# Expert weights in pieces of twice the size, and the arena they live in laid out anew

## The chip, the cores and the metric

The kernel runs on one core of one Trainium2 chip. The metric is device time in microseconds (us), the median of the runs of one kernel. A core has five engines with an instruction sequence each: PE (TensorE, matrix products; its weight loads are listed apart as PEld), DVE (VectorE), ACT (ScalarE), POOL (GpSimd) and SP (SyncE, which here only issues DMAs). They meet through semaphores. Data come from HBM into SBUF (128 partitions) by DMA; matrix products end in PSUM.

## The reference

One decoder block on 256 tokens of width 2048, all in float32. Cut to what matters:

```python
h    = rms_norm(x, norm_mix_g)
proj = h @ w_in                                  # 2048 x 7168
x    = x + concat([moba_attention(q, k, v), hgrn2(q, f, i, g)]) @ w_out
h2   = rms_norm(x, norm_ffn_g)
# router: best of 4 groups, best 2 of its 4 experts -> combine[token, expert]
for e in range(16):                              # 2048 -> 1024 -> 2048
    a, u = h2 @ w_gate[e], h2 @ w_up[e]
    hid  = silu(a) * u * combine[:, e]
    out  = out + hid @ w_down[e]
y    = rms_norm(x + out, final_norm_g)
```

The 16 experts have three matrices of 8 MB each, 24 MB an expert and 384 MB in all. Every one is read once.

## The kernel before

**Front part (0 to about 494 us).** X is normed and transposed, fourteen in-projections and one out-projection run as float32 split into a high and a low half (three products), with attention and HGRN worked off between them from a queue of small steps. The projection weights come in pieces of 1 MB called `raw` (`issue_raw`, L97), two buffers of them. `units()` splits each into two `whl` tiles: ACT copies the high half (L262), DVE subtracts to get the low half (L263), PE uses both. After chosen units (`ahead`) it also issues the load of a piece of expert weights.

**Experts.** Tokens of one expert are gathered into 64 places. For expert e, PE does, in the order of the code: the gate products `ga` (`stream`, L823), the up products `up` (also L823), the scatter of the expert before (L811 into a `psc` buffer, of which there are two, then L813 on DVE adds it into `acc`), a scatter matrix (two transposes, L798), the gather of the next expert (L775 from X into `psc`, L777 on ACT copies to `xn`, L783 transposes, L786 on DVE scales into `xg`), the transposes of `hid` (L871, copied by DVE at L872), and the down products `pd` (L880, copied out by ACT at L883). That is program order; a scheduler then sets the order on each engine, and it weaves L811, L775 and L783 between the products of the next expert. The last expert's down products run in column blocks of 512 (L893 to L913), each followed by its scatter and by the final norm's sums.

**The last norm's gain.** `final_gain()` spreads the 2048 gains of the final norm over all partitions by 16 small matmuls (`pt<-frow`, L836) and four ACT copies (L838). It is called in expert 15, between gate and up.

**Weights.** A matrix is cut into 8 pieces of 1 MB, 8 KB in each partition, loaded by SP (L233 for gate and up, L236 for down; L242 for the last expert's down). SBUF has an arena of 22 slots of 8 KB per partition, `area(s)`. In the front part they hold `hT`, `oT`, attention and HGRN buffers, `raw` and `whl`; each becomes a weight slot when its last front tenant is done. The first 22 pieces go into the 22 slots (`first`); three of these become `acc` (two) and `work` in expert 0, and the other 19 form a ring (`cycle`). When PE has used a piece, `advance()` issues the next load into the slot that has come free.

Of the kernel before, what the change touches and what calls it, by code (L numbers as in the profile page):

```python
# [19 lines left out]
P = 128  # L20
T = 256
# [16 lines left out]
def hybrid_block_kernel(  # L38
# [19 lines left out]
    def area(s, shape, dtype=F32, name="ar"):  # L58

        return arena.tile(shape, dtype, name=name, tag=f"a{s}")  # L60

    def pair(s, name):
        t = area(s, [P, 2, 1024], name=name)
        return t[:, 0], t[:, 1]
# [116 lines left out]
    hTh = [area(0 + i, [P, 8, T], F32R, name="hTh") for i in range(2)]  # L181
    hTl = [area(2 + i, [P, 8, T], F32R, name="hTl") for i in range(2)]
    oTh = [area(4 + i, [P, 8, T], F32R, name="oTh") for i in range(2)]
    oTl = [area(6 + i, [P, 8, T], F32R, name="oTl") for i in range(2)]
# [37 lines left out]
    def slot_of(idx):  # L222
        return first[idx] if idx < NSLOT else cycle[(idx - NSLOT) % len(cycle)]

    def load():
        nonlocal nxt
        e, kind, i = pieces[nxt]
        wt = area(slot_of(nxt), [P, 2048], name="wt")
        if kind < 2:

            src = (w_gate, w_up)[kind][0, e].rearrange("(b p q) f -> p b q f", p=P, q=4)
            q = 2 * (i % 2)
            nc.sync.dma_start(out=wt.rearrange("p (a b) -> p a b", a=2),  # L233
                              in_=src[:, i // 2, q:q + 2, :])
        elif e < NE - 1:
            nc.sync.dma_start(out=wt, in_=w_down[0, e, i * P:(i + 1) * P, :])  # L236
        else:
            b, hf = i // 2, i % 2
            k = 4 if b < 3 else 2
            for a in range(0, 4, k):  # L240
                r0 = (hf * 4 + a) * P
                nc.sync.dma_start(  # L242
                    out=wt.rearrange("p (a b) -> p a b", a=4)[:, a:a + k],
                    in_=w_down[0, e, r0:r0 + k * P, b * 512:(b + 1) * 512].rearrange(
                        "(c p) f -> p c f", p=P))
        loaded[nxt] = wt
        nxt += 1
# [3 lines left out]
    ahead = {12, 20, 100, 104}  # L251
    ahead |= {112 + u for u in (1, 3, 6, 8, 11, 13, 16, 18, 21, 23, 26, 30)}

    def units():
# [5 lines left out]
        for hf in range(2):  # L260
            t = area(19 + unit % 3, [P, 2, k, 1024 // k], F32R, name="whl")
# [296 lines left out]
    def att_block(g, a, hook=None):  # L558
        later = {}
        kT, qT = map(heads, pair(a[0], "kq"))  # L560
        vA, s1 = pair(a[1], "vs")
# [8 lines left out]
        bgq.append(attention(g, qT, kT, s1, area(a[2], [P, 2048], name="asc"), later))  # L570
# [5 lines left out]
    def rec_block(g, a):  # L576
        later = {}
        f, k = map(heads, pair(a[0], "fk"))
# [9 lines left out]
        q, qs = map(heads, pair(a[1], "qq"))  # L588
# [3 lines left out]
        AT, vv = pair(a[2], "av")  # L592
        AT = AT.rearrange("p (h n t) -> p h n t", h=4, n=NT)
        vv = tiles(vv)
        o, sg = pair(a[3], "os")
        later["o_"] = o.rearrange("p (n h e) -> p n h e", n=NT, h=4)
        bgq.append(hgrn(f, k, q, AT, area(a[4], [P, 1536], name="rsc"), later))
# [12 lines left out]
    att_block(0, (8, 9, 10), h_chunks)  # L610
    att_block(1, (11, 12, 13))
    rec_block(0, (14, 8, 9, 10, 11))
    rec_block(1, (12, 13, 14, 8, 9))
# [41 lines left out]
    while nxt < NSLOT:  # L655
        load()
# [96 lines left out]
    def advance():  # L753
        if nxt < len(pieces):
            load()

    def piece(e, kind, i):
        return loaded.pop((e * 3 + kind) * 8 + i)
# [57 lines left out]
    def stream(ps, xg, e, kind):  # L816
        for i in range(8):
            wt = piece(e, kind, i)
            for k in range(2):
                c = 2 * i + k  # L820
                for z in range(2):
                    o = k * 1024 + z * 512
                    mm(ps[64 * z:64 * z + 64], xg[:, c], wt[:, o:o + 512],  # L823
                       start=c == 0, stop=c == NC - 1)
            advance()

    out_v = out[0].rearrange("(n p) d -> p n d", p=P)
    fs = cst.tile([P, NT, 4], F32, name="fs")
    def final_gain():
        sl = [slot_of((NE - 1) * 24 + i) for i in (5, 6, 7)]  # L830
        gf = area(sl[0], [P, D], name="gf")
        y = [area(sl[1 + n], [P, D], name=f"y{n}") for n in range(NT)]
# [6 lines left out]
        return sl, gf, y  # L839
# [5 lines left out]
    for e in range(NE):  # L845
# [17 lines left out]
        V.tensor_tensor(hid, hid, up, ALU.mult)  # L863
        if pend is not None:
            scatter(*pend)
# [4 lines left out]
        for j in range(4):  # L870
            nc.tensor.transpose(pt[:, j], hid[:, j * P:(j + 1) * P], ident)  # L871
        V.tensor_copy(hT, pt)  # L872
        pd = pq.tile([P, 2, 512], F32, name="pd")
        if e < NE - 1:
            for i in range(8):
                wt = piece(e, 2, i)
                z, j = i // 4, i % 4
                for blk in range(4):
                    lo = 64 * (blk % 2)
                    mm(pd[lo:lo + 64, blk // 2], hT[:, j, z * 64:z * 64 + 64],  # L880
                       wt[:, blk * 512:(blk + 1) * 512], start=i == 0, stop=i == 7)
                advance()
# [4 lines left out]
    osl = osb.rearrange("p j (k f) -> p (j k) f", k=2)  # L887
    for b in range(4):
        for hf in range(2):
            wt = piece(NE - 1, 2, 2 * b + hf).rearrange("p (c f) -> p c f", c=4)  # L890
# [36 lines left out]
    with tc.If(nover > CAP):  # L927
        with tc.tile_pool(name="ovp", bufs=1, space=PSUM) as ovp:
            free = [s for s in range(NSLOT) if s not in alias + sl]
            h2T = [area(free.pop(), [P, 8, T], name="h2T") for _ in range(2)]  # L930
            oc = small8[:, 6:8]
            for n in range(NT):
                xs = area(free.pop(), [P, D], name="xs")
                V.tensor_scalar(xs, x2[:, n], r2[:, n:n + 1], None, ALU.mult)
                for c in range(NC):
                    pt = ovp.tile([P, P], F32, name="pt", tag="pt", bufs=2)
                    nc.tensor.transpose(pt, xs[:, c * P:(c + 1) * P], ident)
                    V.tensor_scalar(h2T[c // 8][:, c % 8, n * P:(n + 1) * P], pt,
                                    gffn[:, c:c + 1], None, ALU.mult)
            hTo = area(free.pop(), [P, 8, T], name="hTo")  # L940
            hd = area(free.pop(), [P, NT, 512], name="hd")
            wts = [area(free.pop(), [P, 4, 512], name="wto") for _ in range(4)]
            yo = [area(free.pop(), [P, D], name="yo") for _ in range(NT)]
            with tc.For_i(0, NE, 1) as e:
# [12 lines left out]
                for fb in range(2):  # L957
                    for kind, src in ((0, w_gate), (1, w_up)):
                        ps = ovp.tile([P, NT, 512], F32, name="ps", tag="ps", bufs=2)
                        for c in range(0, NC, 4):  # L960
                            wt = rows4(src, c, fb * 512)
                            for k in range(4):
                                for n in range(NT):
                                    mm(ps[:, n], h2T[c // 8][:, c % 8 + k, n * P:(n + 1) * P],
# [58 lines left out]
```

## Time and profile before

| | us |
|---|---|
| runs | 1428.54, 1429.59, 1430.69 (median 1429.59) |
| profiled execution | 1428.93, with a span of 1427.2 |
| front part, 0 to 494 | PE 483.29 busy, DMA share 0.61 |
| experts 3 to 14, 653 to 1335 | 682.00 long, PE 644.89 busy, PEld 215.21, DMA share 1.01, 421 GB/s |
| the end, 1335 to 1427 | PE 73.27 busy, DMA share 0.85 |

PE carries 94% of the chain that ended last, and its granted clock over the span is 0.996 of full speed, so PE ran at 2.4 GHz. "Idle before" in the rows is the time an engine stood still before a group, with the operation that ended it in the bracket. The matmul rows of the timeline count hardware instructions: one matmul of 512 float32 columns has two of them, one of 128 columns has one.

### The profile page before, as it was taken

What the parts mean: (1) busy time and instruction counts of PE and PEld (TensorE: products, weight loads), DVE (VectorE), ACT (ScalarE), POOL (GpSimd) and SP (SyncE); (2) the same over time, 40 slices, a digit from 0 to 9 for tenths busy, and PEclk for the clock granted to TensorE, in tenths of its full rate; (3) what the DMA queues carried; (4) which work ended last, traced back from release to release, by engine and by line L of the source; (5) the groups of instructions that cost most, each with busy time, mean ns of one, the idle gap of its engine ahead of it and who ended that gap; (6) DMA issues with size and microseconds to landing.
All of it is one profiled execution on the core that took longest, in us unless ns stands there. A gap on an engine that the chain in (4) does not pass through costs nothing.

```text
span 1427.2 us, 16870 instructions
## 1 busy us (share of the span) xinstructions
PE 1357.8 (95%) x7073; PEld 737.6 (52%) x7073; DVE 439.8 (31%) x714; ACT 273.7 (19%) x408; POOL 18.0 (1%) x47
## 2 busy tenths in 40 slices
PE   7999999999999999999999999999999999999995
PEld 6999898898887633433332332323323333233333
DVE  4554557557555410221112111111111111211012
ACT  5453543533533300000000000000000000000012
POOL 2000000000000000000000000000000000000002
PEclk9999999999999999999999999999999999999998
DMA  6566553555697699999999999999999999999995
GB/s 229 186 210 169 162 176 120 176 177 178 219 343 292 228 384 418 422 421 422 420 421 422 421 422 421 422 420 421 421 422 422 420 422 421 421 421 421 421 413 214
DMA packets 111648, 483.79 MB, mean 339 GB/s; under 512 B 19728, under 2 KB 21968, under 8 KB 63440
## 3 DMA queue, kind: packets, MB, share of 16 engines
q1 hardware_dynamic: 110912, 482.62, 85.5%
q8 instruction: 57, 0.93, 0.3%
q14 instruction: 23, 0.19, 0.0%
q10 hardware_dynamic: 656, 0.04, 0.0%
HBM read 480.54 MB, written 2.10 MB: 338 GB/s over the span
## 4 chain that ended last, share of the span: by engine, by line
PE 94%; DVE 2%; ACT 1%; issue 1%; DMA 0%; SPq 0%; DVEq 0%; ACTq 0%
PE ga L823 16%; PE up L823 16%; PE pd L880 15%; PE psc L811 7%; PE pp L310 5%; PE pp L312 5%; PE pp L311 5%; PE pp L293 4%; PE pp L295 4%; PE pp L296 4%; PE psc L775 4%; PE pt L783 1%; PE pw L414 1%; PE pd L893 1%; ACT work L883 1%
## 5 line engine op out<-in xcount | busy, mean ns | idle before, releaser
L823 PE MATMUL ga<-wt,xg 128*64 128x512 f32 x1024 | 272.3, 601 | 0.0
L823 PE MATMUL up<-wt,xg 128*64 128x512 f32 x1024 | 228.0, 595 | 0.0
L263 DVE TENSOR_TENSOR whl<-raw,whl 128x1024 fp32r<-128x1024 f32 x144 | 175.6, 1224 | 136.1 <-ACT whl L262 135.9
L880 PE MATMUL pd<-wt,work 128*64 128x512 f32 x960 | 210.0, 594 | 4.0 <-DVE work L872 4.0
L262 ACT ACTIVATE whl<-raw 128x1024 fp32r<-128x1024 f32 x144 | 152.0, 1058 | 233.4 <-PE pp L312 121.5
L813 DVE TENSOR_TENSOR acc<-acc,psc 128x512 f32<-128x512 f32 x112 | 74.4, 686 | 378.3 <-PE psc L811 378.3
L823 PEld LDWEIGHTS ga<-wt,xg 128*64 128x64 f32 x1024 | 78.8, 136 | 149.0 <-issue 139.8
L293 PE MATMUL pp<-hTh,whl 128*128 128x256 f32 x512 | 147.7, 288 | 3.1 <-ACT hTh L328 3.1
L295 PE MATMUL pp<-hTl,whl 128*128 128x256 f32 x512 | 146.5, 286 | 0.9 <-DVE hTl L329 0.9
L296 PE MATMUL pp<-hTh,whl 128*128 128x256 f32 x512 | 146.2, 286 | 0.0
L823 PEld LDWEIGHTS up<-wt,xg 128*64 128x64 f32 x1024 | 72.5, 137 | 135.0 <-issue 127.7
L880 PEld LDWEIGHTS pd<-wt,work 128*64 128x64 f32 x960 | 69.2, 137 | 134.3 <-issue 123.9
L811 PE MATMUL psc<-work,pT 64*128 64x512 f32 x240 | 99.7, 642 | 16.5 <-ACT work L883 15.4
L293 PEld LDWEIGHTS pp<-hTh,whl 128*128 128x128 f32 x512 | 99.4, 194 | 4.2 <-ACT hTh L328 4.0
L295 PEld LDWEIGHTS pp<-hTl,whl 128*128 128x128 f32 x512 | 99.4, 194 | 1.5 <-DVE hTl L329 1.4
L296 PEld LDWEIGHTS pp<-hTh,whl 128*128 128x128 f32 x512 | 99.4, 194 | 0.0
L883 ACT ACTIVATE work<-pd 128x1024 f32<-128x1024 f32 x15 | 15.3, 1023 | 429.0 <-PE pd L880 429.0
L775 PE MATMUL psc<-X,pg 128*64 128x512 f32 x256 | 94.8, 596 | 0.7 <-DVE pg L767 0.7
L863 DVE TENSOR_TENSOR work<-work,up 128x512 f32<-128x512 f32 x16 | 11.0, 687 | 244.4 <-PE up L823 244.4
L777 ACT ACTIVATE xn<-psc 128x512 f32<-128x512 f32 x32 | 19.0, 595 | 308.2 <-PE psc L775 308.2
L310 PE MATMUL pp<-whl,hTh 128*128 128x512 f32 x192 | 77.6, 404 | 0.0
L312 PE MATMUL pp<-whl,hTl 128*128 128x512 f32 x192 | 75.4, 393 | 0.0
(240 smaller groups left out, 1054.7 us busy)
## 6 DMA issues: line engine op xcount, KB each, us to landing
wt<-in_w_gate_dram SPq DMA_DIRECT2D x128, 1024.0 KB, 19.8
wt<-in_w_up_dram SPq DMA_DIRECT2D x128, 1024.0 KB, 19.8
wt<-in_w_down_dram SPq DMA_DIRECT2D x126, 1024.0 KB, 19.8
raw<-in_w_in_dram SPq DMA_DIRECT2D x55, 1024.0 KB, 5.2
raw<-in_w_out_dram SPq DMA_DIRECT2D x16, 1024.0 KB, 5.3
X<-in_x_dram SPq DMA_DIRECT2D x4, 512.0 KB, 7.1
wt<-in_w_down_dram SPq DMA_DIRECT2D x4, 512.0 KB, 11.4
out_dram<-y SPq DMA_DIRECT2D x4, 512.0 KB, 4.3
```

Source lines behind the costliest of these rows:

```text
L262: S.activation(t[:, 0], raw[:, k * hf:k * hf + k], AF.Copy)
L263: V.tensor_tensor(t[:, 1], raw[:, k * hf:k * hf + k], t[:, 0].bitcast(F32), ALU.subtract)
L293: mm(o, hi[:, k, cs], ah, start=st and j % 2 == 0, stop=False, skip_group_check=True)
L295: mm(o, hi[:, k, cs], al, start=False, stop=False, skip_group_check=True)
L296: mm(o, lo[:, k, cs], ah, start=False, stop=sp, skip_group_check=True)
L310: mm(pp[:, n], ah, hi[:, k], start=c == c0, stop=False)
L312: mm(pp[:, n], al, hi[:, k], start=False, stop=c == c1 - 1)
L775: mm(ps[64 * z:64 * z + 64], pg[:, n], x2[:, n, b * 512:(b + 1) * 512], start=n == 0, stop=n == 1)
L811: mm(ps, pT[lo:lo + 64, n], osb[lo:lo + 64, j], start=True, stop=True)
L813: V.tensor_tensor(acc[n][:, bs], x2[:, n, bs] if e == 0 else acc[n][:, bs], ps, ALU.add)
L823: mm(ps[64 * z:64 * z + 64], xg[:, c], wt[:, o:o + 512], start=c == 0, stop=c == NC - 1)
L880: mm(pd[lo:lo + 64, blk // 2], hT[:, j, z * 64:z * 64 + 64], wt[:, blk * 512:(blk + 1) * 512], start=i == 0, stop=i == 7)
```

## The change

The expert weights come in pieces of 2 MB: four to a matrix, 16 KB in each partition. In gate and up, a partition's four rows of a block are now one load; in down, the rows of a half matrix are dealt to the partitions in fours (`p j` where it was `j p`), so that two neighbouring rows lie in one stretch, and `hid` is transposed with every fourth column (`p j`) to fit. The arena has ten slots of 16 KB (`double`) and two of 8 KB (`single`). Twelve loads (22 MB) go out early: eight after units in the front part (where sixteen did), four behind it. The ring has nine doubles (18 MB), where it had 19 singles (19 MB). `acc[0]` and `work` share a double, `acc[1]` is a single that is freed in expert 1. `final_gain()` runs in expert 1 rather than 15, into the other single.

```diff
+    shared = {k: double(k, [P, 2, 2048], name=f"sh{k}") for k in (1, 2, 3, 8)}
...
-            raw = area(17 + i % 2, [P, k, w], name="raw")
+            raw = half((8, i % 2)).rearrange("p (k w) -> p k w", k=k)
...
-    pieces = [(e, kind, i) for e in range(NE) for kind in range(3) for i in range(8)]
-    first = [15, 16, 10, 11, 0, 1, 2, 3, 12, 13, 9, 14, 8, 4, 6, 17, 18, 5, 7, 19, 20, 21]
-    NSLOT = len(first)
-    alias = first[13:16]
-    cycle = [s for s in first if s not in alias]
+    pieces = [(e, kind, i) for e in range(NE) for kind in range(3) for i in range(4)]
+    early_loads = [(1, 0), (2, 1), (3, 4), (4, 5), (5, 2), (6, 3), (0, 0, 0), (7, 6),
+                   (8, 8), (9, 9), (10, 7), (0, 1, 1)]
+    ring = [d[1] for d in early_loads if len(d) == 2 and d[0] != 7]
+    late_loads = [(11, 0, 0), (11, 1, 1)] + [(n, ring[(n - 12) % 9]) for n in range(12, len(pieces))]
...
+        if kind < 2:
+            return (w_gate, w_up)[kind][0, e].rearrange("(b p q) f -> p b q f", p=P, q=4)[
+                :, i, a:b, :]
+        return w_down[0, e].rearrange("(z p j) d -> p z j d", p=P, j=4)[
+            :, i // 2, i % 2 * 2 + a:i % 2 * 2 + b, :]
...
+        wt = double(at[0], [P, 2, 2048], name="wt")
+        loaded[idx] = [wt[:, 0], wt[:, 1]]
+        if e < NE - 1 or kind == 0:
+            nc.sync.dma_start(out=wt.rearrange("p h (a b) -> p (h a) b", a=r // 2),
+                              in_=source(idx, 0, r))
...
-    ahead = {12, 20, 100, 104}
-    ahead |= {112 + u for u in (1, 3, 6, 8, 11, 13, 16, 18, 21, 23, 26, 30)}
+    ahead = {12, 102, 113, 117, 122, 127, 131, 136}
...
     def stream(ps, xg, e, kind):
-        for i in range(8):
-            wt = piece(e, kind, i)
-            for k in range(2):
-                c = 2 * i + k
+        for i in range(4):
+            for h, wt in enumerate(piece(e, kind, i)):
+                for k in range(2):
+                    c = 4 * i + 2 * h + k
...
-            advance()
+            if (e, kind, i) not in ((0, 0, 0), (0, 1, 3)):
+                advance()
...
-        if e == NE - 1:
-            sl, gf, y = final_gain()
+        if e == 1:
+            gf = final_gain()
...
-            for n in range(NT):
-                acc[n] = area(alias[n], [P, D], name=f"acc{n}")
-            work = area(alias[2], [P, 2048], name="work")
+            rest = double(6, [P, 2, D], name="rest")
+            acc[0] = rest[:, 0]
+            work = rest[:, 1]
...
-            nc.tensor.transpose(pt[:, j], hid[:, j * P:(j + 1) * P], ident)
+            nc.tensor.transpose(pt[:, j], hid.rearrange("s (p j) -> s j p", j=4)[:, j], ident)
...
+    yt = double(late_loads[-9][1], [P, NT, D], name="y")
```

The order of the instructions moves with it, since the scheduler places PE's small work by the loads. On PE, in one of the experts 3 to 14, the stretch from the scatter of the expert before (L811) over the gate products to the transposes of the gathered tokens (L783) reads before:

```order
L880 MATMUL pd<-wt,work 64x512 x32
L811 MATMUL psc<-work,pT 128x512
L823 MATMUL ga<-wt,xg 64x512 x4
L811 MATMUL psc<-work,pT 128x512
L823 MATMUL ga<-wt,xg 64x512 x4
L811 MATMUL psc<-work,pT 128x512 x2
L823 MATMUL ga<-wt,xg 64x512 x4
L811 MATMUL psc<-work,pT 128x512 x2
...
L775 MATMUL psc<-X,pg 64x512
L783 MATMUL pt<-ident,xn 128x128 x4
L823 MATMUL up<-wt,xg 64x512 x4
L783 MATMUL pt<-ident,xn 128x128 x4
```

The same stretch on PE now (L848 is the scatter, L860 the products, L812 the gather, L820 its transposes, L921 the down products; `rest` holds `work`):

```order
L921 MATMUL pd<-wt,rest 64x512 x32
L848 MATMUL psc<-rest,pT 128x512 x2
L860 MATMUL ga<-wt,xg 64x512 x8
L848 MATMUL psc<-rest,pT 128x512 x4
L860 MATMUL ga<-wt,xg 64x512 x8
L848 MATMUL psc<-rest,pT 128x512 x2
L812 MATMUL psc<-X,pg 64x512
L860 MATMUL ga<-wt,xg 64x512 x8
L812 MATMUL psc<-X,pg 64x512 x6
L860 MATMUL ga<-wt,xg 64x512 x8
L812 MATMUL psc<-X,pg 64x512
L820 MATMUL pt<-ident,xn 128x128 x8
```

The eight scatter products went in six places of one or two; they now go in three places of two, four and two, with eight gate products between, and the eight transposes stand in one row where four up products parted them.

On SP, in the out-projection of the front part, the pieces of `raw` (L97) and of expert weights (L233) stand before as:

```order
L97 DMA raw<-in_w_out_dram 128x4x512 x3
L233 DMA wt<-in_w_gate_dram 128x2048
L97 DMA raw<-in_w_out_dram 128x4x512
L233 DMA wt<-in_w_gate_dram 128x2048
L97 DMA raw<-in_w_out_dram 128x4x512
```

and now on SP (`sh_73` is the shared double that holds both `raw` buffers):

```order
L111 DMA sh_73<-in_w_out_dram 128x4x512 x3
L267 DMA wt<-in_w_gate_dram 128x4096
L111 DMA sh_73<-in_w_out_dram 128x4x512 x2
L267 DMA wt<-in_w_up_dram 128x4096
L111 DMA sh_73<-in_w_out_dram 128x4x512 x2
```

Where one 1 MB weight piece stood between two `raw`, one of 2 MB stands between every second or third pair.

## Rows read from the trace of the kernel before

**Rows 1.** The page, part 1: busy time, share of the span, instructions.
```profile
PE 1357.8 (95%) x7073; PEld 737.6 (52%) x7073; DVE 439.8 (31%) x714; ACT 273.7 (19%) x408; POOL 18.0 (1%) x47
```

**Rows 2.** Timeline of PE, one expert: start, us, engine, line, operation, [idle before].
```profile
870.74 13.95 PE L880 MATMUL pd<-wt,work 128*64 128x512 f32 x64 [0.34 <-DVE work L872]
885.88 1.12 PE L811 MATMUL psc<-work,pT 64*128 64x512 f32 x2 [1.18 <-ACT work L883]
886.93 1.94 PE L823 MATMUL ga<-wt,xg 128*64 128x512 f32 x8
888.80 1.12 PE L811 MATMUL psc<-work,pT 64*128 64x512 f32 x2
...
891.72 1.13 PE L811 MATMUL psc<-work,pT 64*128 64x512 f32 x4
...
901.55 0.64 PE L775 MATMUL psc<-X,pg 128*64 128x512 f32 x1
...
910.33 0.75 PE L783 MATMUL pt<-ident,xn 128*128 128x128 f32 x4
911.01 1.94 PE L823 MATMUL up<-wt,xg 128*64 128x512 f32 x8
...
927.41 0.63 PE L871 MATMUL pt<-ident,work 128*128 128x128 f32 x4 [1.61 <-DVE xg L786]
...
928.82 1.51 PE L880 MATMUL pd<-wt,work 128*64 128x512 f32 x6 [0.34 <-DVE work L872]
```

**Rows 3.** Timeline of SP, the same experts: issues of eight loads of down.
```profile
890.25 17.72 SPq L236 DMA_DIRECT2D wt<-in_w_down_dram  x8
949.88 17.71 SPq L236 DMA_DIRECT2D wt<-in_w_down_dram  x8
```

**Rows 4.** Waits of PE's weight loads, 560 to 1300: total, times, longest.
```profile
PEld ga L823 <- DMA wt<-in_w_up_dram: 8.8, 13, 0.8
```

**Rows 5.** Timelines of SP and PE at the end of the last expert.
```profile
1370.33 28.55 SPq L242 DMA_DIRECT2D wt<-in_w_down_dram  x10
1408.49 3.67 PE L893 MATMUL pd<-wt,work 128*64 128x256 f32 x32
```

**Rows 6.** The page, part 6: median us from issue to landing.
```profile
wt<-in_w_down_dram SPq DMA_DIRECT2D x4, 512.0 KB, 11.4
```

**Rows 7.** DMA, 600 to 1300, and GB/s in 40 slices of 1370 to 1428.
```profile
DMA packets 40454, 294.79 MB, mean 421 GB/s; under 512 B 4493, under 2 KB 4493, under 8 KB 4493
GB/s 418 429 418 412 424 412 429 407 400 420 387 384 390 386 381 388 387 387 388 388 387 383 331 254 223 155 49 0 6 0 11 0 11 76 396 401 407 178 6 0
```

**Rows 8.** Timeline of PE, experts 1 and 2: the scatter.
```profile
570.07 1.13 PE L811 MATMUL psc<-work,pT 64*128 64x512 f32 x4
571.97 1.72 PE L811 MATMUL psc<-work,pT 64*128 64x512 f32 x4 [0.77 <-DVE acc L813]
...
617.26 1.13 PE L811 MATMUL psc<-work,pT 64*128 64x512 f32 x4
...
631.78 3.60 PE L775 MATMUL psc<-X,pg 128*64 128x512 f32 x16
```

**Rows 9.** Timeline of ACT, the end of one gather.
```profile
910.89 0.59 ACT L777 ACTIVATE xn<-psc 128x512 f32<-128x512 f32 x1
```

**Rows 10.** Timeline of PE, experts 14 and 15.
```profile
1334.01 0.63 PE L871 MATMUL pt<-ident,work 128*128 128x128 f32 x4 [1.62 <-DVE xg L786]
...
1352.09 1.12 PE L811 MATMUL psc<-work,pT 64*128 64x512 f32 x2 [1.18 <-ACT work L883]
...
1376.56 13.90 PE L823 MATMUL up<-wt,xg 128*64 128x512 f32 x64
```

**Rows 11.** Timelines of SP and ACT, and the tile `raw`, out-projection.
```profile
398.85 0.37 SPq L97 DMA_DIRECT2D raw<-in_w_out_dram  x1
404.66 1.06 ACT L262 ACTIVATE whl<-raw 128x1024 fp32r<-128x1024 f32 x1 [1.66 <-PE pp L312]
DMA to landing us min/median/max: 5.0/5.4/6.4
```

More of the change, by code (lines that the diff above doesn't have):

```diff
@@ L246, in load @@
-        loaded[nxt] = wt
-        nxt += 1
+        idx, *at = loads[nxt]
+        nxt += 1
+        e, kind, i = pieces[idx]
+        r = 4 if kind < 2 else 2
+        if len(at) == 2:
+            hf, s = at
+            wt = single(s, [P, 2048], name="wt")
+            nc.sync.dma_start(out=wt.rearrange("p (a b) -> p a b", a=r // 2),
+                              in_=source(idx, hf * r // 2, (hf + 1) * r // 2))
+            loaded.setdefault(idx, [None, None])[hf] = wt
+            return
+        wt = double(at[0], [P, 2, 2048], name="wt")
@@ new lines, in load @@
+        loaded[idx] = [wt[:, 0], wt[:, 1]]
+        if e < NE - 1 or kind == 0:
+            nc.sync.dma_start(out=wt.rearrange("p h (a b) -> p (h a) b", a=r // 2),
+                              in_=source(idx, 0, r))
+        elif kind == 1:
+            for hf in range(2):
+                nc.sync.dma_start(out=wt[:, hf].rearrange("p (a b) -> p a b", a=2),
+                                  in_=source(idx, 2 * hf, 2 * hf + 2))
+        else:
+            src = w_down[0, e].rearrange("(z p j) d -> p z j d", p=P, j=4)
+            for hf in range(2):
+                k = 4 if i < 3 else 2
+                for a in range(0, 4, k):
+                    nc.sync.dma_start(
+                        out=wt[:, hf].rearrange("p (a b) -> p a b", a=4)[:, a:a + k],
+                        in_=src[:, hf, a:a + k, i * 512:(i + 1) * 512])
@@ L569, in att_block @@
         V.tensor_tensor(qT, ps, rBh, ALU.mult)
-        bgq.append(attention(g, qT, kT, s1, area(a[2], [P, 2048], name="asc"), later))
+        bgq.append(attention(g, qT, kT, s1, half(a[2]), later))
         ps = proj_n(hTh, hTl)
@@ L591, in rec_block @@
         V.tensor_tensor(q, q, qs, ALU.mult)
-        AT, vv = pair(a[2], "av")
+        AT, vv = pair(a[2])
         AT = AT.rearrange("p (h n t) -> p h n t", h=4, n=NT)
         vv = tiles(vv)
-        o, sg = pair(a[3], "os")
+        o, sg = pair(a[3])
         later["o_"] = o.rearrange("p (n h e) -> p n h e", n=NT, h=4)
-        bgq.append(hgrn(f, k, q, AT, area(a[4], [P, 1536], name="rsc"), later))
+        bgq.append(hgrn(f, k, q, AT, half(a[4]), later))
         ps = proj_n(hTh, hTl)
@@ L753, in advance @@
     def advance():
-        if nxt < len(pieces):
+        if nxt < len(loads):
             load()
     def piece(e, kind, i):
-        return loaded.pop((e * 3 + kind) * 8 + i)
+        return loaded.pop((e * 3 + kind) * 4 + i)
     def pscr(tag="psc"):
@@ L829, in final_gain @@
     def final_gain():
-        sl = [slot_of((NE - 1) * 24 + i) for i in (5, 6, 7)]
-        gf = area(sl[0], [P, D], name="gf")
-        y = [area(sl[1 + n], [P, D], name=f"y{n}") for n in range(NT)]
+        gf = single(1, [P, D], name="gf")
         for q in range(4):
@@ L863, in hybrid_block_kernel @@
         V.tensor_tensor(hid, hid, up, ALU.mult)
+        if e == 1:
+            acc[1] = single(0, [P, D], name="acc1")
         if pend is not None:
@@ L874, in hybrid_block_kernel @@
         if e < NE - 1:
[L875 to L882, printed above, removed]
+            for i in range(4):
+                for h, wt in enumerate(piece(e, 2, i)):
+                    z, j = i // 2, i % 2 * 2 + h
+                    for blk in range(4):
+                        lo = 64 * (blk % 2)
+                        mm(pd[lo:lo + 64, blk // 2], hT[:, j, z * 64:z * 64 + 64],
+                           wt[:, blk * 512:(blk + 1) * 512], start=i + h == 0, stop=i + h == 4)
+                if (e, i) != (0, 3):
+                    advance()
             S.activation(osb, pd, AF.Copy)
@@ L928, in hybrid_block_kernel @@
         with tc.tile_pool(name="ovp", bufs=1, space=PSUM) as ovp:
-            free = [s for s in range(NSLOT) if s not in alias + sl]
-            h2T = [area(free.pop(), [P, 8, T], name="h2T") for _ in range(2)]
+            free = [d for d in ring if d != late_loads[-9][1]]
+            h2 = double(free.pop(), [P, NC, T], name="h2T")
             oc = small8[:, 6:8]
+            xss = double(free.pop(), [P, NT, D], name="xs")
             for n in range(NT):
-                xs = area(free.pop(), [P, D], name="xs")
+                xs = xss[:, n]
                 V.tensor_scalar(xs, x2[:, n], r2[:, n:n + 1], None, ALU.mult)
```

102 lines of the change are left out of this document (52 added, 50 removed).

## The prediction

> **What bounds the kernel now.** I read the busy shares first, then the timeline of one expert, then the queue that brings the weights, then the end. PE is busy for 95% of the span, so the reader looks for what PE waits for and what paces it [rows 1]. In experts 3 to 14 all is periodic: the down products begin at 870.74 in one expert and at 928.82 in the next, so the period is 58.08 us [rows 2]. Inside it PE stands still in four places, 1.18 us before the scatter (ACT copies the down products out), 1.61 before the hid transposes (a late release by DVE's gather), 0.34 before the down products, none of them for a weight. Only PE's weight loads, which run ahead of PE, waited for pieces, in the worst group 13 times in 740 us and never over 0.8 us [rows 4].
>
> The queue is nevertheless full: two issues of down lie 59.63 us apart, which is 24 MB at 2.485 us per MB [rows 3], 421 GB/s [rows 7]. DMA is thus 59.63 - 58.08 = 1.55 us an expert slower than PE and lives off the 22 MB that were loaded ahead. This lead is just used up at the end: the last 512 KB are issued at 1370.33 + 28.55 = 1398.88 and land about 11.4 later [rows 5, 6], at 1410.3; the second half of the last block's down products, which needs them, starts at 1408.49 + 3.67/2 = 1410.3 [rows 5]. So PE sets the time, with DMA level with it only at the last half block. A faster DMA alone buys nothing; a slower or later one costs at once.
>
> **The change part by part.** The sum is made against the profiled execution, 1428.93; the median of the runs is 0.66 above that.
>
> *The transfers.* The same bytes in stretches of 16 KB. The traces show 8 KB stretches at 421 GB/s, and 2 KB stretches (the last expert's down) at about 387 [rows 7]. Per engine (one of 16) a stretch of 8 KB takes 311 ns and one of 2 KB 84.7, so 6 KB cost 226.6 and about 9 ns are fixed; one of 16 KB would take 614 ns, 427 GB/s. That is an estimate: 1.5% less, 58.7 to 58.9 us an expert, still not below PE, and over the 900 us in which the queue is full about 13 us earlier at the end. Cashed: 0, since PE is the bound. Bounds: 421 GB/s (if the stretch is cut into 8 KB again) gives 0 as well, but then the lead decides, below.
>
> *The scatter and gather in one expert (12 experts, 3 to 14).* A scatter product of 512 columns uses half the rows, and two in a row run beside each other: a place with one product occupies 886.93 - 885.88 = 1.05, and the rows of one and of two are as long, 1.12 and 1.13 [rows 2]. Four gate products take 888.80 - 886.93 = 1.87; eight in one row about 3.58, since the change of work costs some 0.16 once and a product 0.43. Before, from the first scatter product to the first gather product: 901.55 - 885.88 = 15.67. After, places of two, four and two. The four have only two buffers: in expert 1, where the scatter stands in one row, the next pair starts 571.97 - 570.07 = 1.90 after the first, waiting 0.77 for DVE's add [rows 8]. So 1.06 + 3.58 + (1.90 + 1.65) + 3.58 + 1.90 (a pair, and the gather product behind it waits for a buffer) + 1.71 (four gate products, to come to the same count) = 15.38. That is -0.29 an expert. Bounds: if no buffer wait shows, 15.38 - 0.84 - 0.84 - 0.6 = 13.1, -2.6; if the pairs' waits all come on top, +0.6. I take -0.29, since the row that it rests on is this very sequence: 12 x -0.29 = -3.5.
>
> *The transposes of the gathered tokens.* Four stood before four up products and four behind, so that ACT's second copy to `xn`, 910.89 to 911.48, lay under PE's work [rows 2, 9]. Eight in a row: the first four end by 911.01, the second four wait for that copy, 0.5 with its release, less 0.1 for one change of work less: +0.4 an expert, 12 x 0.4 = +4.8. The cover of four up products (1.87) is what is lost. Bounds 0 and +0.6.
>
> *hid transposes with a stride.* The `xn` transposes, which also take every fourth column, last 0.75 where the hid ones last 0.63 [rows 2]: +0.12 x 16 = +1.9. Bounds 0 and 0.25 each.
>
> *Expert 2.* The scatter stands among the up products. From its first product to the gather 631.78 - 617.26 = 14.52 in five places of two, one, two, two and one with 4 up products between [rows 8]; now three, four and one with eight between. The three and the four each wait for buffers, 2 x 0.84 and more: about 16.4, +1.9. Bounds 0 and 3.
>
> *The gain row.* It goes from expert 15 to expert 1. Expert 14: transposes to scatter took 1352.09 - 1334.01 = 18.08 [rows 10]; elsewhere (928.82 - 927.41) + (885.88 - 870.74) = 16.55 [rows 2], so 1.5 is saved. Expert 15: from the scatter to the up products 1376.56 - 1352.09 = 24.47 [rows 10]. Without the row and with the scatter in twos and fours, 1.06 + 3.58 + 3.55 + 3.58 + 1.06 + 6.9 (16 more gate products) + 0.4 = 20.2: -4.3. In expert 1 the same sixteen small products come to the path, with no work between them: +4.3. Sum -1.5.
>
> *The early loads.* In the out-projection a `raw` is used 404.66 - 398.85 = 5.8 us after its issue, and it lands in 5.4 [rows 11]. Behind a load of 2 MB it would take about 2.3 us more. But ACT's split stands 1.66 behind PE each time [rows 11], and with three split buffers PE holds some 3 us of work in hand: cost 0. If that cover is gone, up to 1 us for each of the seven loads there, +7.
>
> *The lead.* The ring is 18 MB, not 19, and a slot comes free after 2 MB. Where the queue has to wait for a slot, in expert 0, its start can be up to 3 MB later: 3 x 2.485 = 7.5 us. Against it stand the estimated 13 us of the faster stretch: cost 0.
>
> Sum: -3.5 + 4.8 + 1.9 + 1.9 - 1.5 = +3.6, so 1432.5 for the profiled execution and **1433** for the median.
>
> **A rule that speaks against my reading.** The rows show PE busy for 95% and its weight loads for 52% of the span [rows 1]. The Trainium skill, "Perfetto Trace Analysis", section Identifying the Most-Contended Engine, holds that matmul busy share does not tell how near TensorE is to its limit and that the share of weight loads does; by that share PE would have slack, and the full queue would be the bound. By my sum the time is 1433, by that rule it is rival A. The period of 58.08 with no matmul waiting for a weight [rows 2, 4] is against it here.
>
> **The rivals.**
> *A, DMA is the bound.* Then PE's terms vanish in the slack and the 13 us of the faster stretch are gained: 1428.93 - 13.2 + 0.66 = 1416. For it: a full queue and a lead that is just used up [rows 3, 5]. Against it: no weight wait of PE in 740 us. 0.07.
> *B, PE's small waits overlap better.* The scatter in twos and fours loses no buffer wait (-2.6 in place of -0.29 in 12 experts would be -31 and is not credible in full, since a gather product behind needs the same two buffers); a third of it, -0.9 an expert, moves the sum by -7 to about 1426. For it: the places of two are free of cost beside those of one [rows 2]. Against it: the wait of 0.77 in expert 1 [rows 8]. 0.2.
> *C, slower by the lead.* The stretch is cut into 8 KB pieces, the rate stays at 421, and the later start (up to 7.5 us) comes out at the last half block, where there is no slack now [rows 5, 6]. PE's own 3.6 hide as much of it: 1428.93 + 0.66 + 7.5 = 1437. It decides once the late start passes 3.6 us. 0.16.
> *D, the stretch brings no rate and the lead holds.* The time is that of my forecast, 1433, but the queue's period stays 59.63. It is held within the forecast.
>
> **How the numbers follow.** Forecast with D 0.57, A 0.07, B 0.2, C 0.16. The forecast's own range is 1429 to 1437: its terms have bounds of some -3 and +4 together when they don't all fall to one side. To hold 8 in 10 I go down through most of B, to 1422, and up over C, to 1440. About 0.2%, 2.9 us, is what a measurement of this kernel can tell from no change: 1426.7 to 1432.5. Faster: A and some 0.13 of B and a little of the forecast, 0.25. Same: the rest of B and a third of the forecast, 0.27. Slower: 0.48.
>
> **What would show it.** In the trace after: the period of experts 3 to 14 (58.2 by my sum); the scatter's second pair waiting near 0.77 for `acc`; the second four `xn` transposes idle near 0.5 behind ACT; hid transposes of 0.75; no matmul waiting for a weight DMA; the queue at 427 GB/s (or at 421, D); 16.4 us in expert 2; the gain row in one 4.3 us block in expert 1. I am wrong if the period falls below 57.8 (B), if matmuls wait for weights in the last experts (C), or if the end comes 10 us earlier (A).

## The result, and the profile after

The changed kernel takes 1437.04 us (median of 4 runs, 1436.37 to 1437.77), the kernel before 1429.32: a ratio of 1.0053, interval 1.0036 to 1.0070. It is slower, as forecast, and lies 4 us above the 1433 of the forecast. The profiled execution took 1436.37, its span is 1434.6: 7.4 more than before.

The page after, part 1, and the timeline of PE in one expert, which answers to [rows 1, 2]:

```profile
PE 1337.6 (93%) x7073; PEld 735.7 (51%) x7073; DVE 437.1 (30%) x714; ACT 274.1 (19%) x408; POOL 17.8 (1%) x47
```

```profile
879.40 0.72 PE L912 MATMUL pt<-ident,rest 128*128 128x128 f32 x4 [1.62 <-DVE xg L823]
...
880.91 13.95 PE L921 MATMUL pd<-wt,rest 128*64 128x512 f32 x64 [0.43 <-DVE rest L913]
896.04 1.13 PE L848 MATMUL psc<-rest,pT 64*128 64x512 f32 x4 [1.18 <-ACT rest L925]
897.10 3.65 PE L860 MATMUL ga<-wt,xg 128*64 128x512 f32 x16
900.69 1.13 PE L848 MATMUL psc<-rest,pT 64*128 64x512 f32 x4
902.59 1.72 PE L848 MATMUL psc<-rest,pT 64*128 64x512 f32 x4 [0.77 <-DVE acc L850]
...
909.72 0.64 PE L812 MATMUL psc<-X,pg 128*64 128x512 f32 x1 [0.77 <-DVE acc L850]
...
920.23 0.75 PE L820 MATMUL pt<-ident,xn 128*128 128x128 f32 x4
921.43 0.75 PE L820 MATMUL pt<-ident,xn 128*128 128x128 f32 x4 [0.45 <-ACT xn L814]
```

The two waits of 0.77 for a scatter buffer, the 0.45 behind ACT's copy, and the longer hid transposes stand where the forecast put them. From the first scatter product to the gather it is 909.72 - 896.04 = 13.68, and 1.71 for four gate products that now follow: 15.39, against 15.38 forecast.

What was not in the forecast is PE's clock. The timeline of PE in expert 1, and windows on PE around the end of the gain row (columns: us, PE busy, granted clock, DMA share, GB/s):

```profile
557.53 3.88 PE L875 MATMUL pt<-frow,ident 16*128 16x128 f32 x32
561.34 15.65 PE L860 MATMUL up<-wt,xg 128*64 128x512 f32 x64
```

```profile
560.90:561.40 0.50, 0.50 (x7) 0.98 1.00 426
561.40:563.00 1.60, 1.60 (x5) 0.50 1.05 451
563.00:564.70 1.70, 1.70 (x6) 0.50 1.02 434
564.70:565.20 0.50, 0.50 (x4) 0.91 0.84 360
565.20:570.00 4.80, 4.80 (x26) 1.00 1.01 427
```

Behind 3.8 us of the 16 small products of the gain row, which fill 16 of the array's 128 rows, the granted clock is 0.50 (1.2 GHz) for 3.4 us; the 32 up products take 15.65 in place of 13.90 [rows 10]. The profile has one more such fall, at 1056.3 to 1059.7, at the head of the down products of an expert, straight behind the stretch in which PE waits 1.62, transposes, and waits 0.43:

```profile
1055.80:1056.30 0.50, 0.50 (x4) 1.00 1.00 426
1056.30:1058.00 1.70, 1.70 (x8) 0.50 0.97 414
1058.00:1059.60 1.60, 1.60 (x8) 0.50 1.11 471
```

Each costs 3.4 / 2 = 1.7 us. The profile of before has none between 17 us and the quiet tail, which begins at 1416. I call the span less half of this time at half clock (the tail left out) the span at full clock: 1427.2 before, 1434.6 - 3.4 = 1431.2 after, 4.0 more.

The queue, over 600 to 1300, and in 40 slices of 1370 to 1434, which answer to [rows 7]; and SP's loads of down, to [rows 3]:

```profile
DMA packets 20558, 299.42 MB, mean 428 GB/s; under 512 B 2281, under 2 KB 2281, under 8 KB 2281
```

```profile
GB/s 415 420 410 407 410 397 385 381 385 389 385 389 381 387 388 388 376 260 218 138 23 10 0 0 0 0 0 0 0 0 5 0 10 0 10 325 402 407 187 5
```

```profile
894.90 19.70 SPq L267 DMA_DIRECT2D wt<-in_w_down_dram  x4
953.18 19.70 SPq L267 DMA_DIRECT2D wt<-in_w_down_dram  x4
```

Half as many packets move at 428 GB/s (427 forecast), and the issues lie 58.28 apart, which is PE's period. The queue runs dry at about 1405, and PE reaches the last half block at 1417.6: the level finish of before became 12 us of slack, and none of it shortens the run. Among PE's waits from 560 to 1430 there is none of a product for a DMA.

### The profile page after: what moved, and what is told of

The parts are those of the page before. It is cut to its first block, busy times and chain, and to the rows that moved or that the text cites. A ratio compares the mean times of both kernels' runs of the same rounds, so it can differ in the third digit from the quotient of the medians.

```text
span 1434.6 us, 16513 instructions
## 1 busy us (share of the span) xinstructions
PE 1337.6 (93%) x7073; PEld 735.7 (51%) x7073; DVE 437.1 (30%) x714; ACT 274.1 (19%) x408; POOL 17.8 (1%) x47
## 4 chain that ended last, share of the span: by engine, by line
PE 92%; DVE 3%; ACT 2%; issue 1%; DMA 0%; SPq 0%; ACTq 0%; DVEq 0%
PE up L860 16%; PE ga L860 16%; PE pd L921 15%; PE psc L848 5%; PE pp L346 5%; PE pp L347 5%; PE pp L348 5%; PE pp L329 4%; PE pp L331 4%; PE pp L332 4%; PE psc L812 4%; DVE acc L850 1%; PE pw L450 1%; PE pd L937 1%; ACT rest L925 1%
## 5 line engine op out<-in xcount | busy, mean ns | idle before, releaser
L860 PE MATMUL ga<-wt,xg 128*64 128x512 f32 x1024 | 252.9, 596 | 0.0
L860 PE MATMUL up<-wt,xg 128*64 128x512 f32 x1024 | 226.1, 597 | 0.0
L921 PE MATMUL pd<-wt,rest 128*64 128x512 f32 x960 | 211.0, 597 | 5.5 <-DVE rest L913 5.5
L299 DVE TENSOR_TENSOR whl<-sh,whl 128x1024 fp32r<-128x1024 f32 x144 | 175.5, 1224 | 132.3 <-ACT whl L298 125.1
L298 ACT ACTIVATE whl<-sh 128x1024 fp32r<-128x1024 f32 x144 | 152.0, 1058 | 232.8 <-PE pp L348 110.1
L860 PEld LDWEIGHTS ga<-wt,xg 128*64 128x64 f32 x1024 | 78.5, 136 | 145.2 <-issue 143.2
L860 PEld LDWEIGHTS up<-wt,xg 128*64 128x64 f32 x1024 | 72.8, 138 | 142.7 <-issue 140.0
L921 PEld LDWEIGHTS pd<-wt,rest 128*64 128x64 f32 x960 | 67.9, 138 | 139.9 <-issue 129.9
L850 DVE TENSOR_TENSOR rest<-rest,psc 128x512 f32<-128x512 f32 x56 | 36.1, 684 | 252.5 <-PE psc L848 252.5
L848 PE MATMUL psc<-rest,pT 64*128 64x512 f32 x240 | 78.9, 641 | 28.1 <-ACT rest L925 15.4
L925 ACT ACTIVATE rest<-pd 128x1024 f32<-128x1024 f32 x15 | 15.4, 1024 | 434.5 <-PE pd L921 434.5
L812 PE MATMUL psc<-X,pg 128*64 128x512 f32 x256 | 83.3, 596 | 10.0 <-DVE acc L850 9.3
L346 PE MATMUL pp<-whl,hTh 128*128 128x512 f32 x192 | 77.5, 404 | 0.0
L347 PE MATMUL pp<-whl,hTh 128*128 128x512 f32 x192 | 74.9, 390 | 0.0
```

What stands on the lines that cost most here:

```text
L298: S.activation(t[:, 0], raw[:, k * hf:k * hf + k], AF.Copy)
L299: V.tensor_tensor(t[:, 1], raw[:, k * hf:k * hf + k], t[:, 0].bitcast(F32), ALU.subtract)
L346: mm(pp[:, n], ah, hi[:, k], start=c == c0, stop=False)
L347: mm(pp[:, n], ah, lo[:, k], start=False, stop=False)
L812: mm(ps[64 * z:64 * z + 64], pg[:, n], x2[:, n, b * 512:(b + 1) * 512], start=n == 0, stop=n == 1)
L848: mm(ps, pT[lo:lo + 64, n], osb[lo:lo + 64, j], start=True, stop=True)
```

## The experiments

Two theories. **P**: PE's own sequence sets the time, and it lost 4 us by the terms of the sum and the rest by falls of its clock. **L**, rival C of the prediction: the coarser loads and the smaller ring set it. Each version ran in 5 rounds beside the kernel before (ring7 in 1). "Half clock" is the time at 1.2 GHz in the profiled execution, without the quiet tail; "clock" the mean over all runs (37 of the kernel before, beside the versions). Small differences between two spans say little: before_02 and before_fill64 have the front part of the kernel before, and the three profiles reach the first gate product at 494.13, 493.67 and 492.98, with the whole difference made in the first 44 us.

| | median | ratio, interval | clock | span | half clock | span at full clock |
|---|---|---|---|---|---|---|
| before | 1429.3 | | 0.995 | 1427.2 | 0 | 1427.2 |
| after | 1437.0 | 1.0036 to 1.0070 | 0.9935 | 1434.6 | 6.8 | 1431.2 |
| gain_parts | 1437.3 | 1.0037 to 1.0061 | 0.993 | 1435.8 | 10.2 | 1430.7 |
| halves | 1436.9 | 1.0037 to 1.0067 | 0.9925 | 1431.4 | 3.4 | 1429.7 |
| hid_rows | 1438.0 | 1.0034 to 1.0063 | 0.992 | 1437.5 | 17.1 | 1429.0 |
| two_dmas | 1438.0 | 1.0047 to 1.0071 | 0.992 | 1436.3 | 13.6 | 1429.5 |
| four_back | 1432.6 | 0.9999 to 1.0023 | 0.993 | 1431.0 | 10.2 | 1425.9 |
| before_02 | 1439.4 | 1.0045 to 1.0078 | 0.992 | 1437.6 | 10.2 | 1432.5 |
| fill | 1458.1 | 1.0171 to 1.0209 | 0.994 | 1459.8 | 13.6 | 1453.0 |
| four_fill | 1452.8 | 1.0136 to 1.0173 | 0.995 | 1452.7 | 6.8 | 1449.3 |
| fill64 | 1453.9 | 1.0158 to 1.0186 | 0.994 | 1453.7 | 6.8 | 1450.3 |
| before_fill64 | 1447.7 | 1.0112 to 1.0142 | 0.9955 | 1448.1 | 6.8 | 1444.7 |
| best | 1441.9 | 1.0075 to 1.0105 | 0.9945 | 1438.7 | 0 | 1438.7 |
| ring7 | 1439.0 | 1.0048 to 1.0085 | 0.992 | 1439.3 | 17.1 | 1430.7 |

**gain_parts.** The gain row in four parts.

```diff
...
-        if e == 1:
-            gf = final_gain()
+        if e >= 1:
+            final_gain(e - 1)
```

`final_gain` now builds a quarter of the row, four of the 16 products, in each of experts 1 to 4.

> The changed kernel, with the gain row of the last norm built in four parts of four small products, one behind the gate products of each of experts 1 to 4. Theory P (PE's own sequence sets the time, and the clock fell to about half for 3.4 us behind the 3.81 us of small products in expert 1, which cost 1.75 us there): no part is long, the up products of expert 1 take 13.9 us again in place of 15.65, and some of the parts lie in waits that PE has anyway: 1437.0 - 1.8 - up to 1 = 1434.2 to 1435.3. Rival L (the later and coarser loads set the time): nothing that the loads depend on moves, 1437.

The fall in expert 1 is gone (timeline of PE):

```profile
557.49 1.15 PE L878 MATMUL pt<-frow,ident 16*128 16x128 f32 x8
558.58 13.95 PE L860 MATMUL up<-wt,xg 128*64 128x512 f32 x64
```

At full clock it is 0.5 us shorter, but the profile has three other falls, two at the head of down products and one in expert 15, and the time is that of the changed kernel (1434.2 to 1435.3 expected). P missed the time: without the fall in expert 1 the profile has more falls, not fewer. Nor is the place certain. The gain row stands whole in expert 1 in seven profiles, and six have a fall there; that of halves, the next version, has none (timeline of PE):

```profile
555.99 3.88 PE L885 MATMUL pt<-frow,ident 16*128 16x128 f32 x32
559.80 13.95 PE L870 MATMUL up<-wt,xg 128*64 128x512 f32 x64
```

**halves.** Early loads in the out-projection one half at a time.

```diff
...
-    ahead = {12, 102, 113, 117, 122, 127, 131, 136}
+    ahead = {12, 102, 113, 115, 117, 119, 122, 124, 127, 129, 131, 136, 138}
```

The part left out makes each of five 2 MB loads two of 1 MB, the second of which goes out at the next chosen unit.

> The changed kernel, with five of the early 2 MB loads of the out-projection each issued as two of 1 MB, with a piece of projection weights between the two, as the kernel before has it. P: no projection piece lands later than about 5.8 us after its issue, the wait of 3.35 us of ACT at 432.9 goes, and PE's offset of 1.8 us there goes with it: 1437.0 - 1.8 = 1435.2. L: the second halves of early loads come up to 6 us later than in the changed kernel, so the time rises, or stays at 1437.

PE's first gate product starts at 493.69, in the changed kernel at 495.23. From a common point at 415 us PE gains 1.8 there, which is all that was lost, though ACT still waits for a projection piece (timeline of ACT of this kernel):

```profile
433.58 2.01 ACT L308 ACTIVATE whl<-sh 128x1024 fp32r<-128x1024 f32 x2 [3.81 <-DMA sh<-in_w_out_dram]
```

So the late landing was not the price; PE's work in hand covers it. What cost is DVE's order in the changed kernel (timelines of DVE and of PE):

```profile
436.61 0.69 DVE L659 TENSOR_TENSOR X<-X,pp 128x512 f32<-128x512 f32 x1 [5.84 <-PE pp L348]
437.21 1.22 DVE L299 TENSOR_TENSOR whl<-sh,whl 128x1024 fp32r<-128x1024 f32 x1
438.35 0.68 DVE L659 TENSOR_TENSOR X<-X,pp 128x512 f32<-128x512 f32 x1
...
437.35 0.51 PE L673 MATMUL pw<-ident,X 128*128 128x128 f32 x2 [0.56 <-DVE X L659]
438.49 0.50 PE L347 MATMUL pp<-whl,oT 128*128 128x512 f32 x1 [0.63 <-DVE whl L299]
```

The scheduler put the addition L659 ahead of the split L299, whose input ACT had ready at about 434. DVE stood 5.84 us at the addition, and PE waited for the addition and then for the split. In halves (below) both splits come first, as they do in the kernel before, and neither shows a wait of PE from 425 to 447 (timeline of DVE of halves):

```profile
434.67 2.36 DVE L309 TENSOR_TENSOR whl<-sh,whl 128x1024 fp32r<-128x1024 f32 x2 [3.64 <-ACT whl L308]
436.95 1.28 DVE L669 TENSOR_TENSOR X<-X,pp 128x512 f32<-128x512 f32 x2
```

The median stayed at 1436.9 (1435.2 expected), from 1433.1 to 1439.7. The profiled run is the fastest of the six.

**hid_rows.** Down rows as before, plain hid transposes; PE's order is unchanged.

```diff
-        return w_down[0, e].rearrange("(z p j) d -> p z j d", p=P, j=4)[
+        return w_down[0, e].rearrange("(z j p) d -> p z j d", p=P, j=4)[
...
-  nc.tensor.transpose(pt[:, j], hid.rearrange("s (p j) -> s j p", j=4)[:, j], ident)
+  nc.tensor.transpose(pt[:, j], hid[:, j * P:(j + 1) * P], ident)
```

> The changed kernel, with the rows of the down matrices dealt to the partitions as before (each 2 MB load of down then has two stretches of 8 KB) and the hid transposes on 128 neighbouring columns. PE's order is that of the changed kernel. P: the transposes take 0.63 again in place of 0.72 and the wait behind them 0.34 in place of 0.43, 0.17 x 16 = 2.7 us less; the fall of the clock in expert 6 (1.7 us) may go too, since the stretch of waits before it is shorter: 1432.6 to 1434.3, with the down loads nearer 421 GB/s and no weight wait of PE. L: a third of the bytes moves at 421 in place of 428 GB/s, about 0.3 us an expert: 1441.

Timeline of PE, one expert:

```profile
1001.13 0.63 PE L912 MATMUL pt<-ident,rest 128*128 128x128 f32 x4 [1.62 <-DVE xg L823]
...
1002.54 13.95 PE L921 MATMUL pd<-wt,rest 128*64 128x512 f32 x64 [0.34 <-DVE rest L913]
...
1059.31 0.63 PE L912 MATMUL pt<-ident,rest 128*128 128x128 f32 x4 [1.62 <-DVE xg L823]
```

The transposes are 0.63 again, the period is 58.18: 0.10 below the 58.28. At full clock 2.2 us are gained; 17.1 us at half clock (three falls, one of 10.2 us in expert 1) took them back. The quiet stretch between the up and the down products, PE's two waits with the small transposes between them, is shorter here, and that did not stop the falls.

**two_dmas.** Two DMAs of 1 MB for each 2 MB piece.

```diff
-            nc.sync.dma_start(out=wt.rearrange("p h (a b) -> p (h a) b", a=r // 2),
-                              in_=source(idx, 0, r))
+            for hf in range(2):
+                nc.sync.dma_start(out=wt[:, hf].rearrange("p (a b) -> p a b", a=r // 2),
+                                  in_=source(idx, hf * r // 2, (hf + 1) * r // 2))
```

> The changed kernel, with every 2 MB piece loaded by two DMAs of 1 MB (stretches of 8 KB). The scheduler then gives PE the order of the kernel before in experts 2 to 14 (scatter in six places, the gathered tokens' transposes parted by four up products). P: 12 x 0.11 + 2.3 (expert 2) = 3.6 us less, 1433.4; the rate is 421 GB/s, and if PE waits for weights it does so in the last expert only. L: the slower rate and the smaller ring together make PE wait for the last pieces, by 5 us or more, 1437 to 1440.

Timeline of PE, two experts:

```profile
998.59 13.95 PE L922 MATMUL pd<-wt,rest 128*64 128x512 f32 x64 [0.43 <-DVE rest L914]
1013.73 1.12 PE L849 MATMUL psc<-rest,pT 64*128 64x512 f32 x2 [1.19 <-ACT rest L926]
...
1056.77 13.95 PE L922 MATMUL pd<-wt,rest 128*64 128x512 f32 x64 [0.43 <-DVE rest L914]
```

In experts 3 to 14 PE's order is that of before, and the period 58.18, 0.10 above the 58.08 of [rows 2] (the stride) and 0.10 below after's (the order). So the size of a DMA alone decides how the scheduler groups PE's work, and in these experts the order's price is 0.10, not more. Elsewhere the other order gives and takes: expert 2 is 2.1 us shorter, experts 1 and 15 are 0.7 and 1.2 longer. No product waited for a weight, at 421 GB/s and with the small ring: L is out. The median is still 1438.0 (1433.4 expected), with 13.6 us at half clock.

**before_02.** The four versions so far are 0.5 to 2.2 us shorter at full clock than the changed kernel, and none is faster: their medians are 1436.9 to 1438.0. So the next question was what makes the clock fall. In the kernel before, an extra product makes only the period longer.

```diff
+            if kind == 0 and i == 0 and 2 < e:
+                mm(ps[0:64, 0:256], xg[:, 0], wt[:, 0:256], start=True, stop=True)
```

> The kernel before, with one extra product of 256 columns (0.21 us, overwritten by the first gate product) at the head of the gate products of experts 3 to 15, so that its period is that of the changed kernel, 58.29 us; the quiet stretch between up and down products stays as it was. P2a (when the quiet stretch comes decides, and the changed period makes it come at other times): 1429.4 + 13 x 0.21 = 1432.1, and one to two falls of 1.7 us more than before: 1433.5 to 1435.5, clock 0.993 to 0.994. P2b (the quiet stretch must be longer than before's): 1432.1 and a clock of 0.995 to 0.996.

Timeline of PE, and windows around one start of down products:

```profile
870.57 0.63 PE L873 MATMUL pt<-ident,work 128*128 128x128 f32 x4 [1.62 <-DVE xg L786]
...
871.98 1.74 PE L882 MATMUL pd<-wt,work 128*64 128x512 f32 x4 [0.34 <-DVE work L874]
```

```profile
868.00:872.20 4.20, 2.21 (x14) 1.00 1.01 421
872.20:874.00 1.80, 1.80 (x6) 0.52 1.01 419
874.00:875.60 1.60, 1.60 (x6) 0.50 1.05 430
```

The quiet stretch is that of [rows 2] to 0.01 us. The product took 0.43, not 0.21: the period is 58.50. That is 5.3 us in 13 experts; the time rose by 9.9, above the range of P2a, the profile has three falls, and the six runs have clocks of 0.991 to 0.993, where 27 of the 37 runs of before had 0.995 or more. P2a holds in kind: the stretch of before can be followed by a fall as well, and with the longer period, this stretch unchanged, falls come more often.

**fill.** Unread products in the quiet stretch.

```diff
+        if e > 1:
+            with tc.issue_after(up_end):     # the last up product
+                for b in range(3):
+                    mm(ga, ident, x2[:, 0, b * 512:(b + 1) * 512], start=True, stop=True)
...
+            with tc.issue_after(tr.ins):     # the last hid transpose
+                mm(ga, ident, x2[:, 0, 0:512], start=True, stop=True)
```

> The changed kernel, with four products of 512 columns in experts 2 to 15 whose result nobody reads: three in the 1.62 us in which PE waits ahead of the hid transposes, one in the 0.43 us ahead of the down products. Theory P2 (what the changed kernel loses beyond its own sequence, some 3 us, is time at half clock, and the falls answer PE's quiet stretch between the up and the down products): no fall behind that stretch is left, only the one behind the gain row in expert 1, and since the extra products lie in waits they cost under 1.5 us in all: 1432.9 to 1435. Rival L (loads): the extra products change nothing but PE's load, 1437 or more. Rival Q (falls come anywhere, whatever PE does): clock 0.992 to 0.994 as in the changed kernel, 1437 to 1438.5.

**fill64** and **before_fill64** use `ga[0:64]` and `ident[:, 0:64]`, from expert 3 on, in the changed kernel and in the one before.

> The changed kernel, with the unread products in PE's waits again, in experts 3 to 15, but 64 columns wide on the array's side (0.43 us each by the gate products, where those 128 wide took 0.89 in the run before). Three of them (1.29) lie in the wait of 1.62 and one (0.43) in that of 0.43. P2: cost at full clock at most 0.3 us an expert; no fall of the clock behind up products from expert 3 on, so only those of expert 1 are left: clock 0.994 to 0.996, 1432 to 1436. Q: the clock stays at 0.993 and the time at 1437 to 1440.

> The kernel before with the same four unread products in experts 3 to 15. P2: the runs of before that are slow by 2 to 5 us (a clock of 0.992 to 0.995) don't occur any more: 1428.5 to 1431 with a spread under 1.5 us, clock 0.996 to 0.997. Q: the clock and the spread stay those of before (0.992 to 0.997, 1428.3 to 1434).

Timeline of PE of fill64:

```profile
883.62 2.74 PE L906 MATMUL ga<-X,ident 128*64 128x512 f32 x6
886.28 0.75 PE L917 MATMUL pt<-ident,rest 128*128 128x128 f32 x4
886.96 1.07 PE L921 MATMUL ga<-X,ident 128*64 128x512 f32 x2
```

Windows on PE of the same kernel:

```profile
600.00:900.00 300.00, 285.14 (x1248) 1.00 1.00 424
900.00:1200.00 300.00, 284.08 (x1240) 1.00 1.00 422
1200.00:1390.00 190.00, 178.49 (x776) 1.00 1.00 421
```

In all three, and in the two kernels below that have these products too, no profile shows a fall from expert 2 on; eight of the nine profiles without them (all but that of before) show one to three there. What is left lies in expert 1, behind the gain row or in the scatter with its waits of 0.77 and 0.18. The clock of most runs is 0.994 to 0.997. So the falls from expert 2 on are answers to this stretch. On the clock of whole runs alone P2 and Q are not parted for before_fill64: 0.994 to 0.996, in the range of the kernel before. But the products took 0.89 each at either width, 2.66 for three, and pushed 1.1 us past the wait: 1.4 us an expert, far more than the falls cost, and all three lie 16 us or more above the times expected. My price was wrong: the 0.43 of a gate product is that of two which run beside each other (one writes partitions 0 to 63 of the bank, its neighbour 64 to 127), and mine had no such neighbour: those 64 wide all wrote the same half, those 128 wide wrote both.

**four_back** undoes or moves four parts together (the edits of halves, two_dmas and hid_rows, the gain row in parts behind the up products of experts 3 to 6). **four_fill** is that with the products of fill.

> The changed kernel with four parts undone or moved together: pieces loaded by two DMAs of 1 MB, early loads of the out-projection in halves, the rows of down in the old order with plain hid transposes, and the gain row in four parts behind the up products of experts 3 to 6. The arena of ten doubles and the ring of 18 MB stay. P: at full clock each gives what its part cost: front -0.45 against the kernel before, period 58.08, the four parts +0.6 each, the gain row out of experts 14 and 15 -5: 1429.4 - 3 = 1426.4, and few falls of the clock, as before, 1426 to 1428.5. L: a smaller ring at 421 GB/s makes PE wait for the last pieces: 1432 to 1437.

> The kernel with the four parts undone, and the four unread products in PE's waits in experts 2 to 15 besides. P2: as that kernel, and no falls of the clock: 1425 to 1427, clock 0.996 or above, faster than the kernel before. L: as that kernel, 1432 to 1437. Q: falls as often as there.

four_back runs 4.4 us faster than the changed kernel (1432.6, 12 runs), at a ratio of 1.0011 to the kernel before, which its interval does not tell from 1. The median lies in L's range, not in P's, but no product waits for a DMA from 560 to 1430. At full clock its span is 1425.9, 1.3 below before's, where P expected 3. The missing 1.7 lies in the parts of the gain row: experts 3 to 6 are 1.0 to 1.3 longer, where 0.6 was expected. Experts 7 to 14 have the period of before, 58.08, so neither the arena of 16 KB slots nor the ring of 18 MB costs anything by itself. Its profile has three falls. four_fill has none behind expert 1, and loses by the price of the products.

**best** writes the gain row into the gate's PSUM bank within the wait, with fill64's products in the other experts.

> The changed kernel with pieces loaded by two DMAs, early loads in halves, down rows in the old order, the gain row in four parts in the wait ahead of the hid transposes of experts 4 to 7 (written to the gate's PSUM bank, so that no scratch buffer is waited for), and the unread products in that wait in the other experts from 3 on. P2: front -0.45, period 58.1, gain row free where it now lies, 5 us less in experts 14 and 15 than the kernel before: 1424 to 1427, clock 0.995 or above, faster than both kernels. L: PE waits for the last pieces, since the lead of 18 MB at 421 GB/s is too small for a faster PE: 1429 to 1433, with waits of products on weight DMAs in the last expert.

It fails by the same price: no fall in the profile, a span of 1438.7, and a median of 1441.9 where P2 expected 1424 to 1427. Two of its four runs had a clock of 0.992, so not all falls are stopped. No version beat the kernel before.

**ring7.** Two slots fewer.

```diff
-    ... [(n, ring[(n - 12) % 9]) for n in range(12, len(pieces))]
+    ... [(n, ring[(n - 12) % 7]) for n in range(12, len(pieces))]
```

> The changed kernel with a ring of seven doubles (14 MB) in place of nine; PE's order is the same. P: no product waits for a weight, at full clock the span is the same (1431), 1436 to 1438 with the falls. L, the rival C of the prediction: 4 MB less lead make the last pieces up to 4 x 2.485 = 10 us later, 1440 to 1447, with waits on weight DMAs in the last experts.

The waits of PE, 560 to 1430, in total, times, longest:

```profile
PE pt L912 <- DVE xg L823: 19.7, 14, 1.6
PE psc L848 <- ACT rest L925: 15.4, 13, 1.2
PE psc L848 <- DVE acc L850: 11.0, 15, 0.8
```

The rest of the list names no DMA either, and the span at full clock is that of the changed kernel to 0.5 us with 4 MB less. Its two runs, 1437.0 and 1441.0, lie one in P's range and one in L's; the slower is the profiled one, with 17.1 us at half clock. The lead is not what sets the time.

## Why the prediction was right, and where its size was off

By its own steps, at full clock, from the starts of PE's groups in the profiles:

- *Transfers.* 428 GB/s against 427, 12 us of slack, 0 cashed: right. Rival A (DMA is the bound) and rival C (the lead) are out, the latter by ring7 and two_dmas. D did not happen.
- *Experts 3 to 14.* The period went from 58.08 to 58.28, +0.20 against +0.23. The runs part it: the order +0.10 (-0.29 and +0.40 forecast), the stride +0.10 (+0.12).
- *Expert 2.* From its neighbour's down products to its own 53.91 became 56.36, +2.4; +1.9 and the stride were forecast.
- *The gain row.* Expert 1: 3.81 (4.3). Expert 14, from scatter to scatter: 59.62 became 58.28, -1.3 with the +0.20 of the period, so -1.5 as forecast. Expert 15, from the scatter to its first down product: 40.67 became 36.05, -4.6 with the stride, against -4.3. In all -2.3 in place of -1.5.
- *The early loads.* Priced at 0, with 7 as the bound. The landing was covered as I said, but 1.8 us went by DVE's order, which I had not read. In this pair of profiles it is +1.1, since the profiled execution of before was 0.7 later at 31 us. That 0.7 is no work of the change: seven profiles with the front part of after reach the first gate product at 494.85 to 495.32, three with that of before at 492.98 to 494.13.

The sum at full clock is +4.0 against +3.6, and without the 0.7 of the start +4.7. That the two come so near is in part luck: the early loads, priced at 0, came out higher and the gain row lower. **The step that was off is the sum itself, in what it left out**: I took PE's clock as a constant, and the falls in the profile of after cost 3.4 us, half of them straight behind the gain row, which now stands alone. Profiled, 3.6 + 0.4 + 3.4 = 7.4. Rival B (smaller waits) did not show: the buffer waits are 0.77, as in [rows 8]. The measured 1437.0 is also the price of rival C, to the microsecond; the number could not part the two, the trace does, with no wait for a weight and 12 us of slack.

How far the falls explain the medians is less sharp. The mean span less the clock's loss (mean clock against 0.9964, about that of an execution whose only loss is the quiet tail) is 1426.6 before, in 37 runs, and 1431.2 after, in 4: 4.6 apart, where the mean spans, 1428.6 and 1435.4, are 6.8 apart; the medians differ by 7.7. **Open**: what decides whether one given stretch is followed by a fall. Its length alone does not (hid_rows, before_02), and the same gain row is followed by one in six profiles of seven; with a longer period falls come more often (before_02), but no run says how. The kernel before has them too: in 9 of its 37 runs the clock is 0.992 or 0.993 and the time 1431.3 to 1434.3. That it has few is then, as far as these runs show, partly luck of its period; this is argued and not shown.

## What to carry to other kernels

Read the clock with the waits: a short block of small products or a cluster of waits on a PE-bound path can cost twice, once by itself (3.81 us for the gain row) and once by what runs at half clock behind it (1.7), and undoing 1 to 2 us elsewhere may show nothing in the time. Look at every engine's order, not only the busy one's: larger early loads moved an addition ahead of a split on DVE and cost 1.8 us. More bandwidth buys nothing where no product waits for a byte; here it became 12 us of slack.

## What the runs showed of the hardware that was not expected

- The granted clock fell to 0.50 behind 3.8 us of products on 16 of 128 rows (in six profiles of seven), and, in some experts only, behind 3.1 us of waits and transposes; a fall lasted 3.4 us, in some profiles 6.8 or 10.2.
- Two products of 512 float32 columns that write different halves of a bank's partitions take 0.87 together (up products, 13.95 for 32); one that has no such neighbour takes 0.89, whether 64 or 128 columns wide (fill64, fill), and one of 256 columns 0.43 (before_02).
- Stretches of 16 KB moved at 428 GB/s (after, 600 to 1300), of 8 KB at 421 (before, two_dmas, four_back).
